# Heads 3 to 14 of a forgetting-attention layer projected by three wide units instead of six narrow ones

## The chip, the cores and the metric

The kernel runs on one core of one Trainium2 chip. The metric is the device time of one execution in microseconds. The engines are TensorE (PE; its weight loads are PEld), VectorE (DVE), ScalarE (ACT), GpSimd (POOL) and SyncE (SP), which issues most DMAs.

## What is computed

Two decoder layers on a sequence of 512 positions and 2048 features, in fp32. Layer 0 is causal forgetting attention with 16 heads of 128, layer 1 is multi-scale retention with 8 heads of 256 (values 512 wide), in chunks of 128. Each layer has one input projection, a SiLU gate, an output projection and a LayerNorm on `ALPHA * h + y`.

```python
# layer 0, x: (1, 512, 2048)
q, k, v, gate, f_logit = split(x @ w_in)              # 4*2048 + 16 columns
q, k = rms_norm(heads(q), q_gain), rms_norm(heads(k), k_gain)
c = cumsum(log_sigmoid(f_logit + b_f))
s = q @ k.T * 128 ** -0.5 + c[:, None] - c[None, :]   # causal
o = softmax(s) @ v
h = layer_norm(ALPHA * x + (o * silu(gate)) @ w_out, ln_gain[0], ln_bias[0])
# layer 1
q, k, v, gate = split(h @ w_in)                       # 2*2048 + 2*4096 columns
q, k = rotary(q), rotary(k) * 256 ** -0.5
o = retention(q, k, v)                                # chunkwise recurrence with decays per head
y = layer_norm(ALPHA * h + (group_norm(o) * silu(gate)) @ w_out, ln_gain[1], ln_bias[1])
```

## The kernel before

All large products are done in fp32 by parts: `split` (L303) makes a high part of an operand on ScalarE (L305) and the rest on VectorE (L306), and `mm3` (L308) sums three matmuls (L310 to L312). A projection is cut into **units**. A `Unit` multiplies the input's four quarters with four quarters of its weights by seven products, p1 to p7, instead of eight (sums of quarters go in, and the outputs are sums of products); a `Plain` unit does the eight. A **narrow** unit has quarters of 256 columns, 512 columns in all; a **wide** one has quarters of 512, 1024 in all. A **block** is the work of one slot on TensorE: 24 matmuls of 256 columns in a narrow unit (14 blocks in a `Unit`), or 12 of 512 columns in a wide one (28 blocks). Each block's weights are one piece of 128x1024, loaded by SyncE (`w_raw`, `w_q`), on some blocks added to another on VectorE (L575), and split.

The seven products pass through three accumulators in PSUM (`acc`, called x, y, z, each two banks). p1, p5 and p6 are copied by ScalarE into a kept tile (L423); later products are added to these (L446 to L468), and four quarters of output come out, named (m, n). A sink takes each. For the first layer's queries and keys that is `Pair.take` (L987): a pair of heads gets its raw queries and keys (`qk_raw`, rooms in0 and in1) by a ScalarE copy (L994) and the sums of squares by four squares per quarter (L999). `normed` then normalizes and transposes them through PSUM, which empties in0 and in1, and `head` does the attention (softmax on ScalarE and VectorE, small PSUM tiles `mmp`, of which there are two). Gates and values of four heads are one wide unit `vg[g]`. The first layer's order is: pair 0 (a `Plain` unit), vg[0], pair 1, vg[1], pairs 2 and 3, vg[2], pairs 4 and 5, vg[3], pair 6, pair 7 (`Plain`). Heads of pairs 6 and 7 ("quick") are worked on side by side. During pair 6's p7 `other_homes` gives the rooms of the input's forms to the forms of the attention's output, and loads and splits one quarter of the input again (`again`).

The second layer goes head by head: a narrow unit for keys and queries, rotated on VectorE (`rope`, L1609 to L1616), and a wide one for values and gates. Head 0's narrow unit is `Plain`, in two halves (L1549), between which the wide unit's first products stand; its results are copied at L1576. The retention's output is scaled on ScalarE (L1753), transposed by TensorE (L1740) and copied out (L1744, L1745).

The order of all engines is fixed when the program is built, by a planner (`Order`): each block on TensorE is one slot, and side work (tasks started with `spawn`) is put in slots by its cost in VectorE and ScalarE time (`need(act=.., dve=..)`), up to 4.4 and 3.8 us of debt. Each room, accumulator and tile of a ring is counted in `free`; a block that needs a room (`require`) makes the planner run the tasks on, within the same slot, until it is free. Weights are loaded up to nine blocks ahead of their product and split two blocks ahead.

## Time and profile before

| | |
|---|---|
| median of 3 runs | 2405.23 us (2400.59 to 2405.72) |
| profiled execution | 2403.45 us, its span 2401.7 us |
| TensorE busy | 2320.4 us, 97% of the span |
| VectorE / ScalarE / GpSimd busy | 1894.4 / 1216.2 / 160.7 us |
| mean granted TensorE clock | 0.988 |
| DMA | 196 GB/s in the mean |

Times in the rows count from the span's start. A matmul's busy time overlaps with the next one's; the step from start to start tells how fast they follow each other. In brackets stands how long an engine was idle before an operation, and what it waited for last.

### The profile page before, as it was taken

To read this page: it belongs to the slowest core of one execution; us is meant where nothing else is said; L and a number is where in the kernel's file an instruction comes from. 1 tells how busy PE (TensorE), PEld (TensorE's weight loads), DVE (VectorE), ACT (ScalarE), POOL (GpSimd) and SP (SyncE) were. 2 spreads that over 40 slices of the span, in tenths; PEclk is the share of its full clock that TensorE was granted. 3 is DMA by queue.
4 is the path that set the end of the run, shared out by engine and by line. 5 is a ranking of instruction groups with operands and counts; after the bars stand their busy time and mean duration, and the time that the engine had idled before them with its cause. 6 is when DMAs were issued, how large, how long until landed. Compare 5 with 4: busy or idle time off the path is not lost.

```text
span 2401.7 us, 34231 instructions
## 1 busy us (share of the span) xinstructions
PE 2320.4 (97%) x13096; PEld 2014.9 (84%) x13096; DVE 1894.4 (79%) x2483; ACT 1216.2 (51%) x1774; POOL 160.7 (7%) x248
## 2 busy tenths in 40 slices
PE   9999999999999999989899999999999999999995
PEld 9888798798799778878779898888889898777784
DVE  5888778678765656679878888898888889987977
ACT  4556556556555534555354545454544445544533
POOL 0000000000000000010020101010101001011002
PEclk9999999999999999999999999999999999999998
DMA  6355544554544467675575857675665659689778
GB/s 225 123 199 175 164 162 159 175 180 153 185 150 156 134 205 233 221 174 154 175 219 194 246 183 220 206 195 187 209 199 193 210 172 265 211 268 292 242 244 190
DMA packets 184564, 471.16 MB, mean 196 GB/s; under 512 B 17968, under 2 KB 63168, under 8 KB 183888
## 3 DMA queue, kind: packets, MB, share of 16 engines
q1 hardware_dynamic: 159136, 395.29, 49.9%
q0 software_dynamic: 25264, 73.69, 12.2%
q8 instruction: 103, 1.69, 0.3%
q14 instruction: 61, 0.50, 0.1%
HBM read 411.20 MB, written 61.91 MB: 197 GB/s over the span
## 4 chain that ended last, share of the span: by engine, by line
PE 44%; DVE 5%; DMA 3%; issue 2%; ACT 1%; POOL 0%; ACTq 0%; DVEq 0%; POOLq 0%
PE acc L310 13%; PE acc L311 13%; PE acc L312 13%; DVE w_l L306 2%; DMA w_raw<-in_wide 2%; PE mmp L310 1%; PE mmp L311 1%; PE mmp L312 1%; DVE w_q L575 1%; ACT w_h L305 1%; PE mmp L1740 0%; DVE z L1840 0%; DMA y_s<-ny 0%; DMA y_s<-y 0%; DMA z_half<-z_in 0%
## 5 line engine op out<-in xcount | busy, mean ns | idle before, releaser
L305 ACT ACTIVATE w_h<-w_q 128x1024 fp32r<-128x1024 f32 x360 | 380.4, 1059 | 425.5 <-DVE w_q L575 218.3
L310 PE MATMUL acc<-w_h,a 128*128 128x512 f32 (+1 forms) x1536 | 551.4, 359 | 6.2 <-DVE kept L468 3.5
L311 PE MATMUL acc<-w_l,a 128*128 128x512 f32 (+1 forms) x1536 | 545.3, 355 | 1.8 <-DVE w_l L306 1.8
L306 DVE TENSOR_TENSOR w_l<-w_raw,w_h 128x1024 fp32r<-128x1024 f32 x314 | 383.4, 1222 | 206.2 <-ACT w_h L305 205.3
L312 PE MATMUL acc<-w_h,a 128*128 128x512 f32 (+1 forms) x1536 | 545.1, 355 | 0.0
L306 DVE TENSOR_TENSOR w_l<-w_q,w_h 128x1024 fp32r<-128x1024 f32 x360 | 439.3, 1221 | 118.1 <-ACT w_h L305 111.1
L310 PE MATMUL acc<-w_h,s 128*128 128x512 f32 (+1 forms) x1408 | 515.9, 366 | 4.3 <-ACT qk_raw L1576 2.1
L311 PE MATMUL acc<-w_l,s 128*128 128x512 f32 (+1 forms) x1408 | 512.0, 364 | 8.0 <-DVE w_l L306 7.9
L312 PE MATMUL acc<-w_h,s 128*128 128x512 f32 (+1 forms) x1408 | 510.1, 362 | 0.0
L305 ACT ACTIVATE w_h<-w_raw 128x1024 fp32r<-128x1024 f32 x314 | 331.7, 1058 | 346.7 <-PE acc L312 161.5
L310 PEld LDWEIGHTS acc<-w_h,a 128*128 128x128 f32 x1536 | 290.9, 189 | 48.3 <-issue 7.4
L311 PEld LDWEIGHTS acc<-w_l,a 128*128 128x128 f32 x1536 | 291.0, 189 | 42.5 <-DVE w_l L306 4.8
L312 PEld LDWEIGHTS acc<-w_h,a 128*128 128x128 f32 x1536 | 290.8, 189 | 41.2
L311 PEld LDWEIGHTS acc<-w_l,s 128*128 128x128 f32 x1408 | 267.6, 190 | 51.4 <-DVE w_l L306 13.6
L310 PEld LDWEIGHTS acc<-w_h,s 128*128 128x128 f32 x1408 | 267.5, 190 | 44.1 <-ACT w_h L305 3.0
L312 PEld LDWEIGHTS acc<-w_h,s 128*128 128x128 f32 x1408 | 267.4, 190 | 41.2
L575 DVE TENSOR_TENSOR w_q<-w_q,w_raw 128x1024 f32<-128x1024 f32 x216 | 263.2, 1220 | 9.0 <-DMA w_raw<-in_wide 6.5
L310 PE MATMUL acc<-a,w_h 128*128 128x256 f32 x464 | 132.9, 287 | 4.3 <-ACT qk_raw L1576 3.1
L312 PE MATMUL acc<-a,w_l 128*128 128x256 f32 x464 | 132.7, 286 | 0.8 <-DVE w_l L306 0.8
L311 PE MATMUL acc<-a,w_h 128*128 128x256 f32 x464 | 132.5, 286 | 0.0
L312 PE MATMUL acc<-s,w_l 128*128 128x256 f32 x448 | 126.8, 283 | 0.0
L311 PE MATMUL acc<-s,w_h 128*128 128x256 f32 x448 | 126.7, 283 | 0.0
(231 smaller groups left out, 2976.3 us busy)
## 6 DMA issues: line engine op xcount, KB each, us to landing
w_raw<-in_wide SPq DMA_DIRECT2D x321, 512.0 KB, 4.0
w_raw<-in_narrow SPq DMA_DIRECT2D x144, 512.0 KB, 3.7
w_q<-in_wide SPq DMA_DIRECT2D x64, 512.0 KB, 4.6
room<-in_wide SPq DMA_DIRECT2D x47, 512.0 KB, 5.0
w_q<-in_narrow SPq DMA_DIRECT2D x26, 512.0 KB, 4.0
y_s<-ny POOLq DMA_DIRECT2D x48, 256.0 KB, 7.0
y_s<-y POOLq DMA_DIRECT2D x40, 256.0 KB, 5.9
room<-in_narrow SPq DMA_DIRECT2D x18, 512.0 KB, 4.5
```

The source lines that it names most:

```text
L305: nc.scalar.activation(h, src, AF.Copy)
L306: nc.vector.tensor_sub(l, src, f32(h))
L310: nc.tensor.matmul(ps, a[0], b[0], start=start, stop=False, skip_group_check=True)
L311: nc.tensor.matmul(ps, a[0], b[1], start=False, stop=False, skip_group_check=True)
L312: nc.tensor.matmul(ps, a[1], b[0], start=False, stop=stop, skip_group_check=True)
L575: nc.vector.tensor_add(u.chain[c], u.chain[c], t)
```

## The change

Three things.

1. Pairs 1 to 6 (heads 3 to 14) come from three wide units, `both[1]`, `both[3]`, `both[5]`, instead of six narrow ones. Each gives pairs i and i+1. The first pair's part is taken as before; the second pair's part is squared for its own sums, and written to DRAM (`parked`) by GpSimd, three quarters from the kept tile, the last by way of a ScalarE copy (`qk_park`). When the first pair's rooms are empty, `fetch` reads it back into them by two loads on SyncE. The order is now both[1], vg[1], both[3], vg[2], both[5], vg[3], pair 7; the attention of both pairs is spawned at the wide unit's p4.
2. `other_homes` runs in vg[3]'s p7, not in pair 6's; its two loads and splits are two tasks, and the quick heads wait for it.
3. In the second layer head 0's narrow unit takes two accumulators, one for each half; and in head 1's wide unit p5 is kept in k1 as in the later heads, no longer in y0, with p2's blocks between those of p1 and p5.

```diff
+SLOW = (("p1", "p2", "+p5"), ("p6",), ("p3", "p7"), ("p4",))
@@ class Pair
+        def has_room(self):
+            return self.raw or fox["emptied"] == self.i and free["in0"] and free["in1"]
...
+        def take_both(self, other, m, n, tile, done):
+
+            def copy():
+                yield need(act=0.5, until=self.has_room)
+                if self.raw is None:
+                    self.new_raw()
+                    self.new_sums()
+                    other.new_sums()
+                    other.parked = [dram.tile([P, 2, 512], F32, name=f"qk_raw{other.i}{i}") for i in range(2)]
+                nc.scalar.activation(self.raw[m][:, :, n * 256:(n + 1) * 256], tile[:, :, :256], AF.Copy)
+                to = other.parked[m][:, :, n * 256:(n + 1) * 256]
+                last = (m, n) == (1, 0)
+                if last:
+
+                    yield need(act=0.5, tmp=1)
+                    t = tmp("qk_park").rearrange("p (e n) -> p e n", e=2)
+                    nc.scalar.activation(t, tile[:, :, 256:], AF.Copy)
+                    nc.gpsimd.dma_start(to, t)
+                    give("tmp", 3)
+                yield need(act=1.2)
+                self.squares(m, n, tile, 0)
+                self.have += 1
+                yield need(act=1.2)
+                other.squares(m, n, tile, 256)
+                if last:
+                    done()
+                else:
+                    nc.gpsimd.dma_start(to, tile[:, :, 256:])
+                    done(3)
+                other.stored += 1
+
+            spawn(copy(), 0)
+
+        def fetch(self):
+            yield need(until=lambda: self.stored == 4 and self.has_room())
+            self.new_raw()
+            for t, d in zip(self.raw, self.parked):
+                nc.sync.dma_start(t, d)
+            yield need(wait=4)
+            self.have = 4
...
             give("in0")
             give("in1")
+            fox["emptied"] = self.i + 1
...
-    qk = [Unit(narrow, i, p.take) for i, p in enumerate(pairs)]
+    both = {i: Unit(wide, 18 + j, partial(pairs[i].take_both, pairs[i + 1]), u2="k2") for j, i in enumerate((1, 3, 5))}
...
-    for i in range(1, 7):
-        qk[i].run(then={"p4": partial(core, i), **({"p7": lambda: other_homes()} if i == 6 else {})})
-        if i in (1, 3, 5):
-            vg[(i + 1) // 2].run()
+    for i in (1, 3, 5):
+        both[i].run(then={"p4": lambda i=i: (core(i), spawn(pairs[i + 1].fetch()), core(i + 1))})
+        vg[(i + 1) // 2].run(then={"p7": lambda: other_homes()} if i == 5 else {})
...
-                self.qk_unit = Plain(narrow, 8, self.take_qk, lambda: [banks[0]] * 2, rows=False)
+                self.qk_unit = Plain(narrow, 2, self.take_qk, lambda: [banks[0], banks[2]], rows=False)
...
-            if h == 1:
-                self.vg_unit.p5 = "y0"
...
-        h.vg_unit.run(leaves=h.h == RH - 1,
+        h.vg_unit.run(SLOW if h.h == 1 else ORDER, leaves=h.h == RH - 1,
                       then={**then, "p4": lambda h=h, last=last: (spawn(h.retain()), last())})
```

The program has 1008 matmuls fewer (13032 before, 12024 now) and 22 DMAs more; the order moves as follows. Line numbers of the changed kernel are higher: the split is L307 and L308, the matmuls L312 to L314.

ScalarE, first layer, the quarters of pair 1 before: copies into `qk_raw`, and four squares per quarter (L999) between high parts of weights (`w_h`).

```order
L994 ACTIVATE qk_raw<-kept 128x2x256
L305 ACTIVATE w_h<-w_raw 128x1024
L999 ACTIVATE kept,rms_ss<-kept 128x128 x4
L994 ACTIVATE qk_raw<-kept 128x2x256
L305 ACTIVATE w_h<-w_q 128x1024
L999 ACTIVATE kept,rms_ss<-kept 128x128 x4
L305 ACTIVATE w_h<-w_q 128x1024 x2
```

The same engine now, the last two quarters of pairs 1 and 2; L1165 and L1170 are the softmax of pair 0's heads.

```order
L1031 ACTIVATE qk_raw<-kept 128x2x256
L1165 ACTIVATE p<-p,sm 128x512
L1170 ACTIVATE p,sm<-p,sm 128x384
L307 ACTIVATE w_h<-w_q 128x1024
L1019 ACTIVATE kept,rms_ss<-kept 128x128 x4
L1031 ACTIVATE qk_raw<-acc 128x2x256
L307 ACTIVATE w_h<-w_q 128x1024
L1019 ACTIVATE kept,rms_ss<-kept 128x128 x4
L1038 ACTIVATE qk_park<-acc 128x512
L1165 ACTIVATE p<-p,sm 128x384
L307 ACTIVATE w_h<-w_q 128x1024
L1019 ACTIVATE acc,rms_ss<-acc 128x128 x4
```

Each quarter has eight squares, four for each pair, and the last one the copy to the tile from which it goes to DRAM.

SyncE now, behind the first wide unit: the second pair's two loads (L1059) among loads of weights (L563).

```order
L563 DMA w_raw<-in_wide 128x1024
L1120 DMA cb<-c_rows 128x512
L563 DMA w_raw<-in_wide 128x1024 x6
L1059 DMA qk_raw<-qk_raw_1866 128x1024
L1059 DMA qk_raw<-qk_raw_1867 128x1024
L563 DMA w_raw<-in_wide 128x1024 x4
```

They stand between two runs of weight loads; before, no queries or keys went through DRAM.

ScalarE, second layer, head 1's wide unit before: `kept` scaled by `gn_r` and `y`, `ny` are head 0's output, `qk_h` the high parts of head 1's rotated keys and queries, L423 the copy of p1.

```order
L305 ACTIVATE w_h<-w_q 128x1024 x6
L1753 ACTIVATE kept<-kept,gn_r 128x512
L305 ACTIVATE qk_h<-rope 128x2x2x256
L1753 ACTIVATE kept<-kept,gn_r 128x512
L305 ACTIVATE qk_h<-rope 128x2x2x256
L1744 ACTIVATE y<-mmp 128x512
L1745 ACTIVATE ny<-mmp 128x512
L1753 ACTIVATE gate<-gate,gn_r 128x512
L423 ACTIVATE kept<-acc 128x1024
```

And now:

```order
L1810 ACTIVATE kept<-kept,gn_r 128x512
L307 ACTIVATE w_h<-w_q 128x1024
L1810 ACTIVATE kept<-kept,gn_r 128x512
L307 ACTIVATE w_h<-w_raw 128x1024
L1801 ACTIVATE y<-mmp 128x512
L1802 ACTIVATE ny<-mmp 128x512
L1810 ACTIVATE gate<-gate,gn_r 128x512
L307 ACTIVATE qk_h<-rope 128x2x2x256
L307 ACTIVATE w_h<-w_q 128x1024 x2
```

High parts of weights, one per block, now stand between the pieces.

TensorE at that place before: the transposes of head 0's output, and the scores of head 1, between two blocks.

```order
L311 MATMUL acc<-w_l,a_9028 128x512
L312 MATMUL acc<-w_h,a_9029 128x512
L1740 MATMUL mmp<-ident,kept 128x128 x8
L310 MATMUL mmp<-qk_h 128x512
L311 MATMUL mmp<-qk_l,qk_h 128x512
L312 MATMUL mmp<-qk_h,qk_l 128x512
```

And now:

```order
L1797 MATMUL mmp<-ident,kept 128x128 x4
L312 MATMUL acc<-w_h,s_8856 128x512
L313 MATMUL acc<-w_l,s_8856 128x512
L314 MATMUL acc<-w_h,s_8857 128x512
L312 MATMUL acc<-w_h,s_8856 128x512
```

A whole block of 12 matmuls follows the first four transposes, before the next four come.

## Rows read from the trace of the kernel before

**Rows 1.** The page: span, and busy time, share and instructions of each engine.
```profile
span 2401.7 us, 34231 instructions
...
PE 2320.4 (97%) x13096; PEld 2014.9 (84%) x13096; DVE 1894.4 (79%) x2483; ACT 1216.2 (51%) x1774; POOL 160.7 (7%) x248
```

**Rows 2.** Windows: us, then PE, PEld, DVE, ACT, POOL busy, PEclk, DMA, GB/s.
```profile
338.30:527.60 189.30, 185.25 (x1179) 164.89 (x1178) 143.50 (x216) 108.46 (x223) 7.54 (x14) 1.00 0.51 166
527.60:716.90 189.30, 185.27 (x1178) 164.90 (x1177) 143.85 (x216) 109.84 (x225) 6.48 (x12) 1.00 0.50 165
...
1188.00:1212.00 24.00, 10.35 (x36) 7.69 (x35) 17.05 (x25) 9.13 (x12) 2.16 (x4) 0.64 0.60 177
1317.00:1341.00 24.00, 24.00 (x116) 19.85 (x115) 23.52 (x25) 16.24 (x22) 6.96 (x12) 1.00 0.64 213
```

**Rows 3.** TensorE's timeline, first layer: start, us, operation, [idle before <-releaser].
```profile
404.35 0.45 PE L310 MATMUL mmp<-qk_h 128*128 128x384 f32 x1 [1.50 <-ACT pT L1096]
```

**Rows 4.** TensorE's timeline, head 0, first wait; the first and last slow spacing.
```profile
1036.20 0.58 PE L310 MATMUL acc<-a,w_h 128*128 128x256 f32 x1 [3.11 <-ACT qk_raw L1576]
...
1039.13 0.28 PE L311 MATMUL acc<-a,w_h 128*128 128x256 f32 x1
```

**Rows 5.** TensorE's timeline, head 0, second wait; first and last slow spacing.
```profile
1062.82 0.67 PE L310 MATMUL acc<-w_h,s 128*128 128x512 f32 x1 [2.05 <-ACT qk_raw L1576]
...
1066.57 0.39 PE L310 MATMUL acc<-w_h,s 128*128 128x512 f32 x1
```

**Rows 6.** TensorE's timeline, head 1's wide unit.
```profile
1188.91 0.39 PE L312 MATMUL acc<-w_h,a 128*128 128x512 f32 x1
1191.06 0.65 PE L1740 MATMUL mmp<-ident,kept 128*128 128x128 f32 x4 [1.76 <-ACT kept L1753]
1196.83 1.12 PE L1740 MATMUL mmp<-ident,kept 128*128 128x128 f32 x4 [5.12 <-ACT kept L1753]
1204.72 0.79 PE L310 MATMUL mmp<-qk_h 128*128 128x512 f32 x1 [6.78 <-ACT ny L1745]
...
1209.90 0.40 PE L310 MATMUL acc<-w_h,s 128*128 128x512 f32 x1
```

**Rows 7.** TensorE's timeline in a narrow unit: first and last of 27 matmuls.
```profile
359.82 0.28 PE L310 MATMUL acc<-w_h,s 128*128 128x256 f32 x1
...
362.94 0.28 PE L312 MATMUL acc<-w_h,s 128*128 128x256 f32 x1
```

**Rows 8.** TensorE's timeline in a wide unit: first and last of 13 matmuls.
```profile
443.74 0.39 PE L312 MATMUL mmp<-qk_h,qk_l 128*128 128x512 f32 x1
...
446.46 0.39 PE L312 MATMUL acc<-w_h,s 128*128 128x512 f32 x1
```

**Rows 9.** Groups by line and shape, ScalarE, 149 to 716.9 us: busy, mean ns.
```profile
L994 ACT ACTIVATE qk_raw<-kept 128x512 f32<-128x512 f32 x18 | 11.0, 620 | 3.8 <-DVE kept L458 2.5 <-DVE kept L463 1.2
```

**Rows 10.** DMA issues, 149 to 773 us: count, KB each, us to landing.
```profile
w_raw<-in_wide SPq DMA_DIRECT2D x64, 512.0 KB, 3.5
...
values<-kept POOLq DMA_DIRECT2D x6, 512.0 KB, 6.1
...
y_raw<-y_a SPq DMA_DIRECT2D x4, 512.0 KB, 6.0
```

**Rows 11.** Waits of SyncE's queue, 149 to 773 us: total, times, longest.
```profile
SPq L561 <- DVE w_q L575: 143.7, 39, 11.5
```

**Rows 12.** ScalarE's and VectorE's timelines, head 0, first wait.
```profile
1035.08 1.07 ACT L1576 ACTIVATE qk_raw<-acc 128x512 f32<-128x512 f32 x2
...
1033.52 1.22 DVE L306 TENSOR_TENSOR w_l<-w_raw,w_h 128x1024 fp32r<-128x1024 f32 x1
```

**Rows 13.** VectorE's and ScalarE's timelines, head 0, second wait.
```profile
1056.07 1.23 DVE L306 TENSOR_TENSOR w_l<-w_q,w_h 128x1024 fp32r<-128x1024 f32 x1 [0.52 <-ACT w_h L305]
...
1061.70 1.06 ACT L1576 ACTIVATE qk_raw<-acc 128x512 f32<-128x512 f32 x2
```

**Rows 14.** ScalarE's timeline, head 1's wide unit.
```profile
1201.12 1.06 ACT L305 ACTIVATE qk_h<-rope 128x1024 fp32r<-128x1024 f32 x1 [4.35 <-DVE rope L1616]
```

More of the change, by code (lines that the diff above doesn't have):

```diff
@@ L909, in split_x @@
         there.add((q, c))
-    fox = dict(heads=0, norms=0)
+    fox = dict(heads=0, norms=0, emptied=0)
     def forget():
@@ L977, in __init__ @@
             self.raw = None
-            self.have = self.scored = 0
+            self.have = self.stored = self.scored = 0
             self.quick = i >= 6
@@ L1003, in take, with new_raw, new_sums, squares @@
             spawn(copy(), 0)
+        def has_room(self):
+            return self.raw or fox["emptied"] == self.i and free["in0"] and free["in1"]
+        def new_raw(self):
+            take("in0")
+            take("in1")
+            self.raw = [pool.tile([P, 2, 512], F32, name="qk_raw", tag=f"in{i}") for i in range(2)]
+        def new_sums(self):
+            self.ss = pool.tile([P, ST, 4], F32, name="rms_ss", tag="rms_ss", bufs=2)
+        def squares(self, m, n, tile, at):
+            for e in range(2):
+                for h in range(2):
+                    v = tile[:, e, at + h * P:at + (h + 1) * P]
+                    nc.scalar.activation(tile[:, e, h * P:(h + 1) * P], v, AF.Square,
+                                         accum_out=self.ss[:, 2 * m + e, 2 * n + h:2 * n + h + 1])
@@ new lines, in take_both @@
+        def take_both(self, other, m, n, tile, done):
+            def copy():
+                yield need(act=0.5, until=self.has_room)
+                if self.raw is None:
+                    self.new_raw()
+                    self.new_sums()
+                    other.new_sums()
[10 more added lines that the diff above has]
+                yield need(act=1.2)
+                self.squares(m, n, tile, 0)
+                self.have += 1
[8 more added lines that the diff above has]
+            spawn(copy(), 0)
@@ L1056, in head @@
             d0, tag_p = self.room[i]
-            turn = (lambda: fox["heads"] >= 2 * self.i) if self.quick else lambda: fox["heads"] == head
+            turn = (lambda: fox["heads"] >= 2 * self.i and fox.get("homes")) if self.quick else lambda: fox["heads"] == head
             yield need(**{d0: 1}, until=lambda: fox.get("forgot") and turn())
@@ L1313, in other_homes, with again @@
                     s4=(HOME["s4"][0], HOME["a11"][1]))
-        def again():
-            for c in range(2):
-                tags = "k2", "k0", "k1"
-                yield need(until=lambda: any(free[t] for t in tags))
-                tag = next(t for t in tags if free[t])
-                take(tag)
-                t = pool.tile([P, 4, 256], F32, name="x_raw", tag=tag)
-                nc.sync.dma_start(t.rearrange("p a b -> p (a b)"), xq[1, 0, c])
-                yield need(dve=1.14, act=0.97, wait=3)
-                if c == 0:
-                    new_form("x21")
-                split_form("x21", t, 4 * c, 4 * c + 4)
-                give(tag)
-            spawn(fetch("a11", "k2", "k0", "k1"))
-        spawn(again(), 1)
+        def again(c):
+            tags = "k2", "k0", "k1"
+            yield need(until=lambda: any(free[t] for t in tags))
+            tag = next(t for t in tags if free[t])
+            take(tag)
+            t = pool.tile([P, 4, 256], F32, name="x_raw", tag=tag)
+            nc.sync.dma_start(t.rearrange("p a b -> p (a b)"), xq[1, 0, c])
+            yield need(dve=1.14, act=0.97, wait=3)
+            split_form("x21", t, 4 * c, 4 * c + 4)
+            give(tag)
+            if c:
+                spawn(fetch("a11", "k2", "k0", "k1"))
+        new_form("x21")
+        for c in range(2):
+            spawn(again(c), 1)
+        fox["homes"] = True
     def late():
@@ L1345, in two_banks @@
         return a, b
-    Plain(narrow, 7, pairs[7].take, two_banks, kind="x").run(
+    Plain(narrow, 1, pairs[7].take, two_banks, kind="x").run(
         BOTH, then={len(BOTH) // 2 - 1: lambda: spawn(fetch("a21", "k2", "k0", "k1")), len(BOTH) - 1: late})
@@ L1548, in __init__ @@
             if h == 0:
[L1549 removed]
+                self.qk_unit = Plain(narrow, 2, self.take_qk, lambda: [banks[0], banks[2]], rows=False)
             else:
[L1551 removed]
+                self.qk_unit = Unit(narrow, 2 + h, self.take_qk, rows=False, u2="y0")
                 if h == 1:
@@ L1910 @@
     part = lambda w, at, n: w[:, at:at + n]
-    pair = lambda i: side(part(fin, 256 * i, 256), part(fin, D + 256 * i, 256))
-    narrow = [pair(i) for i in range(8)]
+    pair = lambda i, n=256: side(part(fin, 256 * i, n), part(fin, D + 256 * i, n))
+    narrow = [pair(i) for i in (0, 7)]
     narrow += [side(part(rin, D + 256 * h, 256), part(rin, 256 * h, 256)) for h in range(RH)]
@@ L1917 @@
     wide += [part(rout[i * D:(i + 1) * D], 1024 * u, 1024) for i in range(2) for u in range(2)]
+    wide += [pair(i, 512) for i in (1, 3, 5)]
     rot, dec = tables()
```

11 lines of the change are left out of this document (1 added, 10 removed).

## The prediction

> **What bounds the kernel now.** I read the page's busy shares first: TensorE is busy 2320.4 of 2401.7 us, VectorE 79% and ScalarE half of the span [rows 1]. So time is TensorE's work plus the places where TensorE waits, and each part of the change is worth what it takes from one of these two. TensorE's work is read from the starts of its matmuls, not from their busy times, since these overlap. Next I read the stages. In the first layer the work repeats every 189.3 us (two narrow units, one wide unit, four heads), TensorE is busy 185.25 us of it at full clock, and VectorE 143.5 and ScalarE 108.5 us [rows 2]: about 4 us per period are waits, of which the row at 404.35 us is typical, an attention matmul that waits 1.50 us until ScalarE has copied a small PSUM tile [rows 3]. In the second layer the timeline shows three larger waits, in head 0 (1036 and 1063 us) and head 1 (1191 to 1205 us) [rows 4, 5, 6]. These three, and the width of the first layer's units, are what the change touches.
>
> **The three wide units.** Removed: 6 narrow units of 14 blocks of 24 matmuls, 2016 matmuls of 256 columns. Added: 3 wide units of 28 blocks of 12, 1008 of 512 columns. Inside a narrow unit 26 spacings take 3.12 us, 0.120 us each [rows 7]; inside a wide one 12 take 2.72 us, 0.2267 us each [rows 8]. So 28 blocks cost 28 x 24 x 0.120 = 80.64 us as two narrow units and 28 x 12 x 0.2267 = 76.17 us as one wide unit: 4.47 us less, three times, **-13.4 us**. TensorE is the bound in all of it, so this lies on the path. The splits of the weights are 128x1024 per block either way and don't change in number.
>
> A rule speaks against this term. The Trainium skill, page "TensorE: Matmul & The Clock Gate", section "Back-to-back issue gap", gives for an isolated matmul a spacing of N/2.4 + 2.5 ns; two of 256 columns would then cost only 2.5 ns more than one of 512, and 1008 times that is 2.5 us instead of 13.4. By that rule the sum below would be 10.9 us higher; the trace disagrees, its two spacings are both some 13 ns above N/2.4.
>
> **The second pair's way through DRAM.** Added per wide unit: four stores of 256 KB on GpSimd's queue, one more ScalarE copy (0.62 us, by the copy that is there already [rows 9]), and two loads of 512 KB on SyncE's queue; the squares and copies of the pairs are as many as before. Nearest rows: 512 KB written to DRAM by GpSimd land in 6.1 us, 512 KB read back by SyncE in 6.0 us [rows 10]. Neither is waited for by TensorE directly: the second pair is read back a dozen and more blocks (over 30 us) after the first is stored, when the first pair's tiles are empty. Behind the loads on SyncE stand weight loads. SyncE's queue has held such loads back for up to 11.5 us in this layer already [rows 11], and loads are issued up to nine blocks ahead, 9 x 2.72 = 24 us, of which a load uses 3.5 [rows 10]. A fetch may thus wait 20 us for nothing. I put it at **0**, at most 2 us for each of the three.
>
> **Waits of the first layer.** The two pairs' attention now starts together behind one wide unit, the same 4 heads per period. VectorE's load is 76% of a period now and would be 143 of 184.8 us, 77%; ScalarE's goes from 57% to 59%. ScalarE's work is denser behind a wide unit, because each quarter brings eight squares instead of four; by the planner's order and the durations of the rows its backlog there grows from 2.3 to 4.1 us at most. Against blocks of 2.72 us with splits two blocks ahead that is near the edge. Some waits grow, others have a different neighbour. Bounds: all 4 us per period vanish (-12 for three) or they double (+12); I take **+1**. Moving the forms' change of homes from the last narrow unit to the last gates' unit moves two splits (1.2 us of VectorE and 1.06 of ScalarE each) and two loads to a place at the same load: 0, within 2.
>
> **Head 0's banks.** The two halves of its query-key unit used one accumulator; now each has its own. First wait: the second half stands 3.11 us for the copies of the first half's result, then 13 spacings at the lower clock, 2.93 us instead of 1.56 [rows 4], together 4.5. The copies that held the accumulator run at 1035.08, but the next block's low part is subtracted only from 1033.52 to 1034.74 [rows 12]: with a free accumulator TensorE next waits for that. So about 1.5 us of the wait go, with some of the slow spacings: **-2.0** (0.5 to 3.5 us). Second wait, p5 of the wide unit for the second half's copies: 2.05 us idle, and 9 spacings in 3.75 us instead of 2.04 [rows 5]; the low part there had been ready since 1057.3, and only the copies at 1061.70 were missing [rows 13]. Nothing is late next: **-3.9** (3 to 4 us).
>
> **Head 1's p5 in another room.** In the kernel before, p5 of head 1's wide unit needed room y0, which two pieces of earlier work still held; the planner pressed all of that work, head 0's last four transposed groups and head 1's rotations and their splits, into one block. TensorE ends its last matmul before that about 1189.1 and starts normal work at 1204.72; between lie only eight transposes, at most 0.12 us each [rows 6], so 15.6 - 0.9 = 14.7 us idle. VectorE and ScalarE work in turns there: the split of the second rotated part ends on ScalarE at 1202.18 [rows 14]. Then 12 spacings at the lower clock take 5.18 instead of 2.72 us [rows 6]: 2.5 more. Together 17.2 us. In the changed kernel the same work is spread over eleven blocks, with no more than 4.5 us of VectorE in any. How that fares is shown by the same place in head 2 (1317 to 1341 us): VectorE busy 23.52 of 24.00 us, TensorE without an idle moment, clock 1.00 [rows 2]. But here VectorE gets 39.0 us (counted over the order, by the rows' durations) in blocks that take TensorE 36.2; its backlog reaches 4.9 us where head 2 reaches 4.2, and the splits are two blocks, 5.4 us, ahead. I leave 1 us of waits: **-16.2** (10 to 17).
>
> **Sum.** -13.4 + 0 + 1 - 2.0 - 3.9 - 16.2 = -34.5 us. The profiled execution took 2403.45 us (span 2401.7), so 2369.0; it lies 1.8 us under the median of the runs, so 2370.7 against that. I say **2370**.
>
> **Rivals.**
> 1. *The wait of head 1 moves.* k1, p5's new room, is freed only once the rotation has read head 1's second pair, and ScalarE's copy into it would stand in front of the splits. For it: VectorE's backlog of 4.9 us at just that place. Against: head 2 does this at nearly the same density without a wait. It would give back 5 to 10 us: 2375 to 2380, taken as 2377.
> 2. *The first layer becomes bound by ScalarE and VectorE.* If each period's waits grow by 5 us (4.1 us of backlog, and the typical wait of 1.5 us three times over), 15 us return: about 2385. For it: two pairs' squares, norms and softmax steps now come in one bunch, and a PSUM bank with the last quarter stays held for about ten ScalarE instructions. Against: average loads of 77% and 59%.
> 3. *Slower.* The fetch waits on SyncE for the transposes that empty the first pair's tiles, and all weight loads stand behind it. It costs nothing up to about 20 us of waiting; to turn -34.5 into a loss, each of three fetches would have to hold the queue some 12 us beyond that, 32 us. Price at 35 us: 3 x (35 - 20) = +45, 2415. For it: SyncE waited 11.5 us for VectorE already [rows 11]. Against: the order puts the fetch behind the emptying tiles' last reader with blocks to spare.
> 4. *Width brings only 2.5 ns per pair of matmuls.* As a mechanism here: the new blocks would run at 0.2375 us a matmul, where the old wide ones show 0.2267 [rows 8]; 2381. By the page named above it would be so; the rows bear it out in no block.
> 5. *It doesn't do what it says*: the planner places the mends where another ring makes them wait, and only the width pays: 2390.
>
> **How the numbers follow.** Forecast 0.66 (2357 to 2376), rival 1 0.12, rival 2 0.12, rival 3 0.04, rival 4 0.01, rival 5 0.05. The range takes the forecast with its bounds, -12 and -2 of the first layer's waits and the mends at the low end, and rival 1 and the nearer part of rival 2 at the high end: 2355 to 2384. 0.2%, 4.8 us, is about what a measurement of this kernel can tell from no change. Faster by more: 0.94, all cases but rival 3 and the far tail of rival 5, to which I give 0.02 within. Slower: 0.04, rival 3.
>
> **What would show it.** The period of the first layer at about 184.8 us plus what its waits changed; 512-column spacing of 0.227 us in the new units; no TensorE wait over 2 us near the second layer's first units and clock 1.00 there; head 1's wide unit as long as head 2's to 1 us. Wrong it would be if rows with waits for a fetched pair, for SyncE's loads or for ScalarE's copies in the first layer add up to more than 10 us, or if head 1's p5 waits for k1.

## The result and the profile after

The changed kernel takes 2382.59 us (median of 4 runs, 2381.26 to 2384.26) against 2405.02 (2400.59 to 2405.72): a ratio of 0.9911, interval 0.9894 to 0.9928. It is 22 us faster; 34.5 were forecast. The time lies inside the range, at its upper end, and 12 us of the gain that the sum gave are missing. The forecast's own bounds ended at 2376; the range reached 2384 because rival 1 and part of rival 2 were added to it. Neither came about as it was described, so that the range holds the time is in part luck.

The page of the changed kernel, the lines that answer to [rows 1]:

```profile
span 2381.5 us, 32252 instructions
...
PE 2304.4 (97%) x12088; PEld 1955.2 (82%) x12088; DVE 1893.1 (79%) x2474; ACT 1212.8 (51%) x1756; POOL 168.9 (7%) x260
```

Where the 20.2 us between the two spans went is found by cutting both timelines at the same blocks (start of the first matmul of each; us):

| stretch | before | after | difference |
|---|---|---|---|
| first period: pairs 1 and 2, vg[1] | 190.3 | 189.5 | -0.8 |
| second period: pairs 3 and 4, vg[2] | 189.7 | 189.0 | -0.7 |
| third period: pairs 5 and 6, vg[3] | 189.3 | 194.8 | +5.5 |
| pair 7 | 54.8 | 60.2 | +5.5 |
| first output projection, LayerNorm, up to head 0 | 205.3 | 200.9 | -4.4 |
| head 0's units and head 1's narrow unit | 196.8 | 189.7 | -7.1 |
| head 1's wide unit | 100.2 | 82.9 | -17.3 |
| all the rest | 1126.0 | 1125.0 | -1.0 |

So the second layer gave 24 us, and the first layer, where TensorE has 13.4 us less to do, became 5 us longer. The windows of the changed kernel for the three periods and the middle of head 1's wide unit (us; PE, PEld, DVE, ACT, POOL busy; PEclk; DMA; GB/s), which answer to [rows 2]:

```profile
149.40:338.90 189.50, 181.21 (x829) 146.07 (x828) 150.85 (x234) 109.69 (x218) 7.64 (x13) 0.99 0.53 178
338.90:527.90 189.00, 181.44 (x839) 146.33 (x838) 144.33 (x213) 107.72 (x217) 9.25 (x16) 1.00 0.55 178
527.90:722.70 194.80, 184.78 (x844) 149.60 (x843) 144.78 (x213) 108.21 (x215) 9.29 (x16) 0.98 0.50 169
...
1171.10:1210.00 38.90, 38.90 (x181) 32.24 (x180) 38.21 (x59) 25.87 (x33) 10.36 (x16) 1.00 0.67 217
```

In the second period TensorE is busy 181.44 us where it was 185.25, so the width is there; but it is idle 7.6 us where it was 4.05. In head 1 the idle time is gone. TensorE's waits by what ended them, 149.4 to 783 us (total, times, longest), the five largest, and behind them the two largest of the kernel before (149.3 to 773.4 us):

```profile
PE mmp L1132 <- ACT pT L1155: 4.5, 4, 2.3
PE acc L313 <- DVE w_l L308: 3.9, 4, 1.1
PE mmp L1091 <- DVE sm L1181: 3.8, 1, 3.8
PE mmp L1277 <- DVE sm L1181: 2.9, 2, 1.5
PE mmp L1132 <- DVE qk_l L1083: 2.6, 2, 2.2
```

```profile
PE mmp L310 <- ACT pT L1096: 4.6, 3, 1.6
PE mmp L1073 <- ACT pT L1096: 2.1, 8, 0.3
```

Four of the five are waits of small products (`mmp`) for ScalarE or VectorE. Over the whole lists the waits that a step of ScalarE ended last fall from 9.0 to 6.2 us, and those that a step of VectorE ended last (`sm`, `qk_l`, `o`, `kept`, `w_l`) rise from 3.3 to 19.0. The timelines show where: these are TensorE's small products, ScalarE's copies and VectorE's steps at the end of vg[2] and the start of the next wide unit.

```profile
513.81 0.60 PE L1100 MATMUL mmp<-ident,qk_raw 128*128 128x128 f32 x4
...
521.09 0.60 PE L1132 MATMUL mmp<-ident,p 128*128 128x128 f32 x4
522.75 0.63 PE L1100 MATMUL mmp<-ident,qk_raw 128*128 128x128 f32 x4 [1.06 <-DVE sm L1171]
527.62 0.55 PE L1132 MATMUL mmp<-ident,p 128*128 128x128 f32 x3 [1.48 <-ACT pT L1155]
530.76 0.60 PE L1100 MATMUL mmp<-ident,qk_raw 128*128 128x128 f32 x4
536.36 0.87 PE L1132 MATMUL mmp<-ident,p 128*128 128x128 f32 x3 [2.23 <-DVE qk_l L1083]
```

```profile
523.42 0.47 ACT L1082 ACTIVATE qk_h<-mmp,cols 128x256 fp32r<-128x256 f32 x1 [0.26 <-PE mmp L1100]
525.42 0.47 ACT L1082 ACTIVATE qk_h<-mmp,cols 128x256 fp32r<-128x256 f32 x1 [1.53 <-DVE qk_l L1083]
...
526.99 0.58 ACT L1155 ACTIVATE pT<-mmp 128x512 f32<-128x512 f32 x1
```

```profile
523.78 1.22 DVE L308 TENSOR_TENSOR w_l<-w_q,w_h 128x1024 fp32r<-128x1024 f32 x1
524.91 0.48 DVE L1083 SCALAR_TENSOR_TENSOR qk_l<-mmp,cols,qk_h 128x256 fp32r<-128x256 f32 x1
```

L1100 transposes the second pair (pair 4, just fetched), L1132 the softmax's result for pair 3's second head; the two alternate. Each group holds one of the two small PSUM tiles (`mmp`) until ScalarE and VectorE have taken it in turns: copy, subtraction, copy, subtraction. VectorE does its first subtraction (524.91) behind a PSUM addition and a split, so ScalarE stands 1.53 us in the middle of the group, and the copy of pT, for which TensorE waits at 527.62, stands behind it.

### The profile page after: what moved, and what is told of

It is laid out like the page before. It is cut to its first block, busy times and chain, and to the rows that moved or that the text cites. A ratio compares the mean times of both kernels' runs of the same rounds, so it can differ in the third digit from the quotient of the medians.

```text
span 2381.5 us, 32252 instructions
## 1 busy us (share of the span) xinstructions
PE 2304.4 (97%) x12088; PEld 1955.2 (82%) x12088; DVE 1893.1 (79%) x2474; ACT 1212.8 (51%) x1756; POOL 168.9 (7%) x260
## 4 chain that ended last, share of the span: by engine, by line
PE 52%; DVE 7%; DMA 5%; issue 3%; ACT 3%; POOL 0%; DVEq 0%; ACTq 0%; SPq 0%; POOLq 0%
PE acc L312 16%; PE acc L314 16%; PE acc L313 16%; DVE w_l L308 2%; DMA w_raw<-in_wide 2%; ACT w_h L307 2%; PE mmp L312 1%; PE mmp L313 1%; PE mmp L314 1%; DMA v_sum<-in_wide 1%; DVE w_q L577 1%; PE mmp L1797 1%; PE mmp L1277 0%; DMA y_s<-ny 0%; DVE z L1897 0%
## 5 line engine op out<-in xcount | busy, mean ns | idle before, releaser
L307 ACT ACTIVATE w_h<-w_q 128x1024 fp32r<-128x1024 f32 x360 | 380.7, 1059 | 433.6 <-DVE w_q L577 232.8
L308 DVE TENSOR_TENSOR w_l<-w_raw,w_h 128x1024 fp32r<-128x1024 f32 x314 | 383.6, 1222 | 195.2 <-ACT w_h L307 193.8
L312 PE MATMUL acc<-w_h,a 128*128 128x512 f32 (+1 forms) x1392 | 528.5, 380 | 6.8 <-DVE kept L470 4.8
L308 DVE TENSOR_TENSOR w_l<-w_q,w_h 128x1024 fp32r<-128x1024 f32 x360 | 439.7, 1222 | 109.4 <-ACT w_h L307 100.7
L313 PE MATMUL acc<-w_l,a 128*128 128x512 f32 (+1 forms) x1392 | 521.3, 375 | 2.1 <-DVE w_l L308 1.9
L314 PE MATMUL acc<-w_h,a 128*128 128x512 f32 (+1 forms) x1392 | 520.8, 374 | 0.0
L307 ACT ACTIVATE w_h<-w_raw 128x1024 fp32r<-128x1024 f32 x314 | 331.8, 1058 | 359.3 <-PE acc L314 168.4
L313 PE MATMUL acc<-w_l,s 128*128 128x512 f32 x1216 | 476.1, 392 | 12.2 <-DVE w_l L308 12.0
L312 PE MATMUL acc<-w_h,s 128*128 128x512 f32 x1216 | 479.7, 394 | 2.5 <-ACT w_h L307 2.5
L314 PE MATMUL acc<-w_h,s 128*128 128x512 f32 x1216 | 474.5, 390 | 0.0
L312 PEld LDWEIGHTS acc<-w_h,a 128*128 128x128 f32 x1392 | 263.5, 189 | 55.3 <-issue 8.7
L313 PEld LDWEIGHTS acc<-w_l,a 128*128 128x128 f32 x1392 | 263.7, 189 | 49.0 <-DVE w_l L308 6.1
L314 PEld LDWEIGHTS acc<-w_h,a 128*128 128x128 f32 x1392 | 263.3, 189 | 47.1
L313 PEld LDWEIGHTS acc<-w_l,s 128*128 128x128 f32 x1216 | 228.6, 188 | 64.7 <-DVE w_l L308 20.4
L312 PEld LDWEIGHTS acc<-w_h,s 128*128 128x128 f32 x1216 | 228.5, 188 | 48.7 <-ACT w_h L307 3.8
L314 PEld LDWEIGHTS acc<-w_h,s 128*128 128x128 f32 x1216 | 228.3, 188 | 48.1
L314 PE MATMUL acc<-a,w_l 128*128 128x256 f32 x464 | 131.7, 284 | 1.7 <-DVE w_l L308 1.7
L312 PE MATMUL acc<-a,w_h 128*128 128x256 f32 x464 | 131.6, 284 | 1.5 <-ACT w_h L307 1.5
L314 PE MATMUL acc<-s,w_l 128*128 128x256 f32 x448 | 126.8, 283 | 0.0
```

The source lines that it names most:

```text
L307: nc.scalar.activation(h, src, AF.Copy)
L308: nc.vector.tensor_sub(l, src, f32(h))
L312: nc.tensor.matmul(ps, a[0], b[0], start=start, stop=False, skip_group_check=True)
L313: nc.tensor.matmul(ps, a[0], b[1], start=False, stop=False, skip_group_check=True)
L314: nc.tensor.matmul(ps, a[1], b[0], start=False, stop=stop, skip_group_check=True)
```

## The experiments

All times are medians of 4 runs or more, each with its ratio to the kernel before on the same chip. The runs are spread over several chips, on which the kernel before took 2402.8 to 2406.5 us, so a difference between two medians is good to some 3 us. The stretch behind head 1 alone takes between 1123.7 and 1130.6 us in the traces, without any edit there. Where small differences matter, the same stretch of two traces is therefore compared too.

**The two parts apart.** e1_mends is the kernel before with the second layer's part alone:

```diff
-                self.qk_unit = Plain(narrow, 8, self.take_qk, lambda: [banks[0]] * 2, rows=False)
+                self.qk_unit = Plain(narrow, 8, self.take_qk, lambda: [banks[0], banks[2]], rows=False)
...
-            if h == 1:
-                self.vg_unit.p5 = "y0"
...
-        h.vg_unit.run(leaves=h.h == RH - 1,
+        h.vg_unit.run(SLOW if h.h == 1 else ORDER, leaves=h.h == RH - 1,
```

> The kernel before with the third part of the change alone: head 0's two accumulators, head 1's p5 in k1 with p2's blocks between. Theory W (the two traces side by side: the wide units save 13.4 us of TensorE but the first layer's waits grow by 20, so the first layer pays nothing, and the whole gain is the mends: head 0's blocks 7.2 us shorter, head 1's 17.2): 2405.0 - 24.4 = 2380.6, as fast as the changed kernel (2382.6) or a little faster. Rival F (the forecast's own terms: mends -22.1, wide units -12.4): 2383, with the first layer's first stretch, 149 to 773 us, as before; but then the changed kernel should have been at 2370. Both agree on the mends within 2 us; W falls if this run is above 2390.

2380.22 us, ratio 0.9898 (0.9882 to 0.9913). e2_wide undoes the same lines in the changed kernel:

> The changed kernel without its third part: head 0's narrow unit in one accumulator, head 1's p5 in y0 in the old order; the wide units and the forms' move stay. Theory W: 2382.6 + 24.4 = 2407, no faster than the kernel before (2405). Rival F (wide units worth 12 us, which something in the mends gave back): 2393.

2406.57 us, ratio 1.0011 (1.0002 to 1.0021): no faster than before. So the whole gain of the change is the second layer's few lines, and the three wide units, as they stood, bring nothing. e7_head1 has head 1's lines only:

> The kernel before with head 1's mend alone (p5 in k1, p2's blocks between). By the traces of before and after head 1's blocks lost 17.2 us of waits: 2402.8 to 2405 less 17.2 = 2386 to 2388, and head 0's two accumulators make the rest up to e1_mends (2380), 6 to 7 us. Rival (the two depend on one another): above 2392 or below 2383.

2388.14 us, ratio 0.9928 (0.9913 to 0.9943), 16.7 us under the kernel before; up to e1_mends 7.9 are left for head 0's accumulators (7.2 by the ratios). In its trace head 1's wide unit takes 82.3 us and head 0's stretch 196.5, as before, so the one part does not hang on the other.

**Is it the way through DRAM?** e4_notrip leaves out the twelve stores, and its fetch loads something that waits for no store; heads 5, 6, 9, 10, 13 and 14 work on other numbers.

```diff
-                    nc.gpsimd.dma_start(to, t)
...
-                    nc.gpsimd.dma_start(to, tile[:, :, 256:])
...
-            for t, d in zip(self.raw, self.parked):
-                nc.sync.dma_start(t, d)
+            for i, t in enumerate(self.raw):
+                nc.sync.dma_start(t.rearrange("p a b -> p (a b)"), wide[0, 0, 0, i])
```

> The changed kernel without the way through DRAM: the stores of the second pairs are left out, and the fetch loads two pieces of a weight instead, so that it waits for no store; heads 5, 6, 9, 10, 13 and 14 thus work on other numbers in the same amount. Theory W with M or L (no wait of TensorE comes from the stores or the fetch): 2382.6 within 3 us. Rival T (part of the 20 us is the round trip, by the kept tiles' later release or by DMA traffic): 2375 or less.

2383.16 us: unchanged. The round trip costs nothing that can be measured.

**The second pair's place.** In e3_later the second pair is normalized and transposed only after the first pair's attention:

```diff
-            yield need(until=lambda: self.have == 4 and fox["norms"] == self.i)
+            yield need(until=lambda: self.have == 4 and fox["norms"] == self.i
+                       and (self.i not in (2, 4, 6) or fox["heads"] >= 2 * self.i))
```

> The changed kernel; the second pair of each wide unit (pairs 2, 4, 6) is normalized and transposed only when both heads of the first pair are through their softmax. Theory M (the waits come where the second pair's transposes and the first pair's attention stand side by side and share the two small PSUM tiles, at the end of the gates' unit and the start of the next): the first layer's waits fall from 43 to some 25 us, 2382.6 - 15 = 2367, with the stretch 149 to 783 us some 15 us shorter. Rival L (it is the load of VectorE in the gates' unit's last products, whichever tasks make it): waits move but keep their sum, 2378 to 2390.

2365.32 us, ratio 0.9832 (0.9818 to 0.9847): 17.3 us faster than the changed kernel, and faster than both kernels that the case compares. Its windows, three periods:

```profile
149.80:333.80 184.00, 179.35 (x821) 145.40 (x820) 144.49 (x214) 107.72 (x215) 7.62 (x13) 0.99 0.56 183
333.80:515.80 182.00, 180.89 (x842) 146.97 (x840) 143.34 (x213) 107.20 (x215) 8.16 (x14) 1.00 0.54 181
515.80:701.10 185.30, 181.67 (x842) 146.86 (x841) 145.08 (x215) 109.52 (x221) 9.67 (x17) 1.00 0.53 178
```

The second period is 7 us shorter than in the changed kernel, with nearly the same busy times; only the idle time has gone. At the same place TensorE's attention now runs by itself, with waits of 0.26 and 0.36 us where they were 1.06 to 2.23:

```profile
507.74 0.60 PE L1133 MATMUL mmp<-ident,p 128*128 128x128 f32 x4
...
511.89 0.55 PE L1133 MATMUL mmp<-ident,p 128*128 128x128 f32 x3 [0.36 <-ACT pT L1156]
515.46 0.55 PE L1133 MATMUL mmp<-ident,p 128*128 128x128 f32 x3 [0.26 <-ACT pT L1156]
```

e8_all_later gives the same condition to all pairs, 1 to 7.

> The changed kernel with every pair from 1 to 7 normalized and transposed only when the heads of the pair before are through their softmax. Theory M: the first pairs' transposes are mostly later than that anyway, so 2361 to 2366, like e3_later or a little less. Rival (attention then runs late, and the end of the first layer or a full room makes TensorE wait): above 2370.

2366.79 us (2365.81 to 2373.25): like e3_later, just above its forecast. The odd pairs were not in the way.

**What is it at that place: load, turns or tiles?** Three kernels put idle work back into e3_later where the transposes had been. e5_load: ScalarE and VectorE work in the same amount, on the two halves of a row of the raw tile one after the other, so that ScalarE's second copy need not wait for VectorE.

```diff
+            if self.i in (2, 4, 6):
+                yield need(until=lambda: self.have == 4 and fox["norms"] == self.i)
+                for s in range(ST):
+                    yield need(act=0.75, dve=0.7)
+                    for h in range(2):
+                        v = self.raw[s // 2][:, s % 2, h * 256:(h + 1) * 256]
+                        nc.scalar.activation(v, v, AF.Copy)
+                        nc.vector.tensor_scalar(v, v, 1.0, None, op0=ALU.mult)
```

> e3_later with idle work put where the second pair's transposes were taken from: when the second pair is in, four steps of two ScalarE copies and two VectorE multiplications by one, 128x256 each, on its raw tile (values unchanged), in place of the two copies and two subtractions of each of the four transposed groups. No PSUM tile and no TensorE work in it. Theory M (the two small PSUM tiles, shared by the transposes and the attention, made the waits): at most 4 us more than e3_later's 2365.3, so 2365 to 2370. Rival L (it was VectorE's and ScalarE's load there): most of the 17 us come back, 2378 or more.

2366.17 us: the load alone is worth 1 us by the medians, and 2.9 by the traces (table below). e9_tiles does it on a small PSUM tile that TensorE has filled, with the old group's shape of turns:

```diff
+                        t = mmp()
+                        for h in range(2):
+                            nc.tensor.transpose(t[:, h * P:(h + 1) * P], self.raw[s // 2][:, s % 2, h * P:(h + 1) * P], ident)
...
+                        for h in range(2):
+                            nc.scalar.activation(last[:, :256], last[:, :256], AF.Copy)
+                            nc.vector.tensor_scalar(last[:, :256], last[:, :256], 1.0, None, op0=ALU.mult)
+                        give("mmp")
```

> e3_later with an idle copy of the old transposes at their old place: when the second pair is in, four groups of two transposes of its raw tile into a small PSUM tile (its 128 columns twice, half of a real group), and one slot later two ScalarE copies and two VectorE multiplications by one of that tile in place, whose result nobody reads. TensorE gets 3 x 4 x 2 x 0.11 = 2.6 us more. Theory M (sharing the two small PSUM tiles with the attention makes the waits): 2365.3 + 2.6 and most of the 17 us, 2378 to 2388. Rival (neither load nor tiles; it was the moment at which the pair's attention could begin): 2366 to 2370.

2381.82 us: 16.5 us come back, of which 2.6 are the idle transposes' own. Its waits on TensorE in the first layer are of the changed kernel's kind again (149.5 to 782 us, the largest three):

```profile
PE mmp L1150 <- ACT pT L1173: 7.3, 7, 2.3
PE mmp L1150 <- DVE o L1309: 1.9, 1, 1.9
PE mmp L312 <- ACT pT L1173: 1.7, 2, 1.3
```

e9_tiles differs from e5_load in two things, the tiles and the turns. e11_turns has the turns alone, with the same order of operations on TensorE, ScalarE and VectorE as e5_load:

```diff
-                    for h in range(2):
-                        v = self.raw[s // 2][:, s % 2, h * 256:(h + 1) * 256]
+                    v = self.raw[s // 2][:, s % 2, :256]
+                    for h in range(2):
                         nc.scalar.activation(v, v, AF.Copy)
```

> e5_load with one thing changed: the two ScalarE copies and the two VectorE multiplications of a step now work in turns on the same 128x256 of the raw tile, so that the second copy waits for the first multiplication, as the second qk_h copy of a transposed group waits for the first subtraction (1.53 us at 525.42 in the changed kernel). No PSUM tile. e9_tiles had both, e5_load neither. Theory M (the small PSUM tiles being held is what costs): 2365 to 2369, like e5_load. Theory C (ScalarE, waiting for VectorE's turn, holds up the attention's copies queued behind it): 2375 to 2384, like e9_tiles.

2373.41 us, between the two forecasts: 7.2 us above e5_load, 8.4 under e9_tiles. e12_parts comes from the other side: it takes the turns out of the changed kernel.

```diff
-                for i, gain in ((0, gq), (2, gk)):
-                    h, l = (p[:, i:i + 2, s * P:(s + 1) * P] for p in self.qk)
+                parts = [(i, gain, *(p[:, i:i + 2, s * P:(s + 1) * P] for p in self.qk)) for i, gain in ((0, gq), (2, gk))]
+                for i, gain, h, l in parts:
                     nc.scalar.activation(h, t[:, i:i + 2], AF.Copy, scale=gain)
+                for i, gain, h, l in parts:
                     nc.vector.scalar_tensor_tensor(l, t[:, i:i + 2], gain, f32(h), op0=ALU.mult, op1=ALU.subtract)
```

> The changed kernel with the two ScalarE copies of a transposed group (query and key high parts) issued before its two VectorE subtractions, in place of copy, subtraction, copy, subtraction; in all pairs; the places in the order stay. Theory C (the second copy's wait for VectorE in the middle of the group is what costs): 2368 to 2376. Theory M (the group's and the attention's tiles together are too many for two): 2380 to 2383, unchanged.

2372.79 us, 9.8 us under the changed kernel. On each of the three engines the operations stand in the same order in both kernels. What differs is the order in which the program issues them: in the changed kernel the second copy, into one part of the tile `qk_h`, waits for the first subtraction, which reads another part of it; no value needs this wait. The groups by line show that the turns were what it removed; ScalarE's `qk_h` copies in the changed kernel (338.9 to 722.7 us) and in e12_parts (330 to 712 us), the idle time before them behind the second bar:

```profile
L1082 ACT ACTIVATE qk_h<-mmp,cols 128x256 fp32r<-128x256 f32 x34 | 16.0, 470 | 33.7 <-DVE qk_l L1083 24.9 <-PE mmp L1091 8.5 <-PE mmp L1100 0.3
```

```profile
L1082 ACT ACTIVATE qk_h<-mmp,cols 128x256 fp32r<-128x256 f32 x34 | 14.1, 465 | 9.1 <-PE mmp L1092 8.9 <-PE mmp L1101 0.3
```

24.9 us in which ScalarE stood for VectorE's subtraction are gone. The traces can be compared by the stretch from the start of the first period to head 0, which holds all that these edits touch:

| kernel | us |
|---|---|
| e3_later | 814.1 |
| e5_load (load) | 817.0 |
| e11_turns (load and turns) | 821.6 |
| e9_tiles (load, turns, tiles) | 831.4 |
| changed kernel | 834.5 |
| e12_parts (changed kernel without the turns) | 820.8 |

So both turns and tiles are at work, but their shares are not settled: the turns are worth 7 to 10 us of the 17 by the medians, and by the traces 4.6 (put in) to 13.7 (taken out) of 20.3. From e11_turns to e9_tiles it is 9.8 us, of which 2.6 are the idle transposes; but the planner counts the small tiles, so the order of operations changes there too, and the tiles' waits are not told apart from that. The one kernel that has the tiles without the turns is e12_parts, 7.5 us above e3_later (6.6 by the traces). It was not tried whether e12_parts and e3_later together give more than e3_later.

**What the width is worth by itself.** For that the narrow kernel has to be without such waits too. e6_narrow_later is e1_mends with e3_later's condition.

> e1_mends (narrow units, both mends) with the same later normalization of pairs 2, 4 and 6 as in e3_later. Tells what the width is worth when the attention stands alike. Theory W+M (width is worth up to 13.4 us once its waits are gone; the narrow kernel too has some of these waits, row 404.35 and its like): 2370 to 2379, that is 5 to 13 us slower than e3_later. Rival (the later normalization alone makes the gain and the width is worth nothing): 2365 to 2367.

2380.09 us, the same as e1_mends and outside both forecasts. But the run tells nothing of the width: in the narrow kernel it is the odd pairs whose transposes alternate with the attention, and the condition for pairs 2, 4 and 6 left the order of operations on TensorE, ScalarE and VectorE exactly as it was. e10_narrow_all has the condition for all pairs, after which no transposes stand among the attention:

> e1_mends (narrow units, both mends) with every pair normalized and transposed only after the heads of the pair before are through their softmax. In e6_narrow_later the delay of pairs 2, 4 and 6 had left the order nearly as it was, since in the narrow kernel it is pairs 3 and 5 whose transposes stand among the attention; here no transposes stand there in any pair, as in e3_later, so the two differ by the width alone. Theory W+M: 2370 to 2379, 5 to 13 us above e3_later (2365.3), and below e1_mends (2380.2). Rival 1 (the width is worth nothing in like orders): 2365 to 2367. Rival 2 (the narrow kernel's waits are not of this kind): 2380.

2372.77 us, ratio 0.9863 (0.9847 to 0.9880): 7.5 us under e1_mends, so the narrow kernel had the same kind of wait, and 7.5 above e3_later. Its windows against those of e3_later above:

```profile
149.00:337.40 188.40, 183.43 (x1165) 163.93 (x1164) 147.78 (x221) 109.10 (x213) 5.95 (x11) 1.00 0.50 171
337.40:524.10 186.70, 185.41 (x1182) 165.56 (x1181) 144.20 (x216) 108.99 (x221) 6.47 (x12) 1.00 0.49 170
524.10:710.40 186.30, 185.04 (x1178) 165.16 (x1177) 142.82 (x215) 110.77 (x225) 6.47 (x12) 1.00 0.49 167
```

Against e3_later a wide unit saves 4.4 and 4.7 us in the first two periods, and 1.0 in the third. But e3_later delays only pairs 2, 4 and 6. The wide kernel with the same condition as e10_narrow_all is e8_all_later, 6.0 us under it; its periods take 181.9, 186.1 and 185.2 us in the profiled execution (the longest of its four), which is 6.5, 0.6 and 1.1 us less. How much attention falls into a period differs between these orders, so no single period gives the price of the width. Together the three periods save 10.1 us (e3_later) or 8.2 (e8_all_later), and up to head 0 it is 7.2 or 3.6.

## Why the prediction was right and wrong, step by step

- **The bound, and the place of the three large waits**: right. TensorE is 97% busy in both, and each term but the first layer's waits was worth about what it was taken to take from TensorE's work or waits.
- **The three wide units, -13.4**: the unit price was right. The new units run at the wide spacing (ten spacings in 2.27 us, TensorE's timeline in both[3], as in [rows 8]); that two periods of e3_later give 4.4 and 4.7 us where 4.47 were worked out agrees with it, but is in part chance, since e8_all_later gives 6.5 and 0.6:

```profile
349.77 0.39 PE L313 MATMUL acc<-w_l,s 128*128 128x512 f32 x1
...
352.04 0.40 PE L314 MATMUL acc<-w_h,s 128*128 128x512 f32 x1
```

  The Trainium skill's formula for an isolated matmul (page "TensorE: Matmul & The Clock Gate", section "Back-to-back issue gap") would have given, as an estimate, 0.8 us per unit; the spacings of the trace disagree, 0.120 us at 256 columns and 0.227 at 512. By that formula the narrow matmul would be the shorter one (an estimate of 0.109 us), and not the wide one the longer, so rival 4's 0.2375 us is not what the formula gives. In sum e3_later is 7.5 us below e10_narrow_all and e8_all_later 6.0, not 13.4; for e3_later the rest is in the third period and pair 7, below.
- **The way through DRAM, 0**: right, by e4_notrip. The loads landed in 5.0 us and the stores in 2.7, where 6 was taken; SyncE had no wait at the fetch itself (L1059). The weight loads of the wide units (L563) waited at most 9.3 us, for a low part, within the 20 that were free; SyncE's longest wait, 14.5 us, stood at a weight load of pair 7 (L718). The changed kernel's DMA groups (149 to 783 us), and these two waits of SyncE:

```profile
qk_raw<-qk_raw SPq DMA_DIRECT2D x6, 512.0 KB, 5.0
...
qk_raw<-kept POOLq DMA_DIRECT2D x9, 256.0 KB, 2.7
```

```profile
SPq L563 <- DVE w_l L308: 145.2, 46, 9.3
...
SPq L718 <- DVE w_l L308: 48.0, 8, 14.5
```

- **Waits of the first layer, +1 (-12 to +12)**: this step failed: the waits grew by 20 us, outside its bounds, and that is more than all that is missing, since some 5 us came back elsewhere (the sum, below). Counted over the starts (each step beyond the spacing of its width, between the start of the first period and the end of pair 7), the waits grew from 22.9 to 43.2 us. The step reasoned from two sums, the average load of VectorE and ScalarE and their backlog. Neither explains these waits: e3_later has the same loads and is 17 us faster, and e5_load adds the load without the wait. It is a chain: a transposed group that ScalarE and VectorE take in turns, the attention's copies behind it on ScalarE, two small tiles for both, and the projection's matmuls behind TensorE's waiting product. The row shown for the typical wait [rows 3] was one end of such a chain (a pT copy), and the prediction did not ask what had held that copy up; the change put pair i+1's transposes, by the fetch, exactly beside pair i's attention. The prediction's sign of being wrong missed it too: it counted waits for a fetched pair, for SyncE's loads and for ScalarE's copies, and these stay under 10 us (6.2 for ScalarE), while those for VectorE grew to 19.0.
- **Rival 2** had the right place and nearly the right size (about 15 us, 2385), but not the cause: it blamed squares, norms and softmax in one bunch, and e3_later keeps all that work, and loses the waits by moving only the second pair's norms and transposes behind the attention.
- **The forms' change of homes, 0 within 2**: not tried alone. The third period, in which it now stands, is 5.8 us longer than the second, and in e3_later 3.3; pair 7 is 5.5 longer than before, and 4.4 come back behind it. From e10_narrow_all to e3_later all up to head 0 gained 7.2 us, where three units should give 13.4; so some 6 us went in the third period and behind it. In the longest wait of the first layer, TensorE's 3.76 us up to 713.16, one of the moved splits takes part: VectorE does it right before the softmax step that TensorE waits for.

```profile
710.46 1.22 DVE L308 TENSOR_TENSOR x<-x_raw,x 128x1024 fp32r<-128x1024 f32 x1
```

  How much of the 6 us is this work and how much the last pairs' attention stays open.
- **Head 0's accumulators, -5.9**: the mechanism was right, -7.1 by the blocks' starts (-7.9 by the medians of e7_head1 and e1_mends, -7.2 by their ratios). The second wait went whole, 3.9 us (its rows add up to 3.8). Of the first wait and its slow spacings 2.9 us went where 2.0 were taken. Some 1 us of the 7.1 has nothing to do with the change: at the start of head 0's unit two short waits of like length (0.8 and 1.2 us) were followed by the lower clock in the kernel before (granted 0.78 from 978.6 to 983 us) and by the higher one in the changed kernel (1.00 from 983.8 to 988); other steps took nearly as much back. The waits in head 0 that are left (984 to 1085 us) are those for VectorE's low parts and ScalarE's high parts, as was said, and one for ScalarE on the forms of the second layer's input (`raw`); `qk_raw` is not among them:

```profile
PE acc L314 <- DVE w_l L308: 1.7, 2, 0.9
PE acc L312 <- ACT w_h L307: 1.5, 2, 1.3
PE mmp L1535 <- ACT raw L1553: 1.2, 1, 1.2
PE acc L313 <- DVE w_l L308: 0.9, 2, 0.6
```

- **Head 1's p5, -16.2**: right, 16.7 by e7_head1 and 17.3 by the starts. The 1 us that was left for VectorE's backlog was not needed, and rival 1 did not occur: VectorE is busy 38.21 of 38.90 us there (above), and TensorE has no idle moment. The transposes that were pressed into one block stand apart now:

```profile
1181.74 0.60 PE L1797 MATMUL mmp<-ident,kept 128*128 128x128 f32 x4
1184.95 0.60 PE L1797 MATMUL mmp<-ident,kept 128*128 128x128 f32 x4
```

- **The sum**: with the measured sizes, -13.4 + 20.3 for the first layer, -7.1 and -17.3 for the heads, 2.5 of TensorE's work moved into the first layer, -4.4 behind it and -1.0 in the rest: -20.4, against -20.2 of the spans.

## What to carry to other kernels

A faster unit on the bounding engine is worth its arithmetic only if the small work between its blocks keeps its own place: when two chains of small steps (here one pair's transposes and another's attention) come to stand side by side and share two PSUM tiles and two engines in turns, the bounding engine waits although no other engine is near full. To forecast such a change, look for what is newly interleaved in the order, and follow one short wait of the kind back through the queues, rather than adding up loads. Of two engines that work on one tile in turns, let the first do all its steps before the second begins; where a chain can start later without being needed sooner, start it later.

## What the runs showed of the hardware

The length of a short wait does not by itself tell at which clock TensorE goes on. In the changed kernel the matmuls behind the waits of 1.06 and 1.48 us (522.75 and 527.62, above) kept the spacing of the higher clock, while behind 2.23 us (536.36) and behind 3.76 us (713.16) they ran at the lower one, 0.427 us a matmul of 512 columns. The granted clock was 0.50 from 536.9 to 539.5 us and 0.52 behind the longer wait; over the whole third period, where both stand, the mean is 0.98. TensorE's timeline behind the longer one, and its window:

```profile
713.16 0.78 PE L1091 MATMUL mmp<-ident,qk_raw 128*128 128x128 f32 x4 [3.76 <-DVE sm L1181]
...
715.02 0.63 PE L312 MATMUL acc<-w_h,a 128*128 128x512 f32 x1
715.45 0.63 PE L313 MATMUL acc<-w_l,a 128*128 128x512 f32 x1
...
717.08 0.39 PE L314 MATMUL acc<-w_h,a 128*128 128x512 f32 x1
```

```profile
713.60:717.10 3.50, 3.50 (x12) 2.77 (x10) 1.61 (x3) 2.57 (x4) 0.00 (x0) 0.52 0.00 0
```

From 713.60 to 717.08 eight spacings take 3.48 us instead of 1.81, so this wait cost 1.7 us more than its own length. But a wait of 2.20 us, at the same transposes and for the same step of VectorE, was followed by the higher clock in e3_later (1.00) and by the lower one in e8_all_later (0.50), first in e3_later:

```profile
720.98 0.63 PE L1092 MATMUL mmp<-ident,qk_raw 128*128 128x128 f32 x4 [2.20 <-DVE qk_l L1084]
```

```profile
720.90:724.00 3.10, 3.02 (x26) 3.05 (x27) 1.30 (x3) 0.95 (x2) 0.00 (x0) 1.00 0.03 5
```

And in e8_all_later:

```profile
721.82 1.09 PE L1091 MATMUL mmp<-ident,qk_raw 128*128 128x128 f32 x4 [2.20 <-DVE qk_l L1083]
```

```profile
721.80:724.90 3.10, 3.08 (x15) 3.10 (x16) 0.91 (x3) 0.95 (x2) 0.00 (x0) 0.50 0.02 5
```

In the same way a wait of 2.3 us for a pT copy early in the first period was followed by seven slow spacings in the changed kernel (at 251.58) and by none in e12_parts (at 249.19). What decides between the two is not shown here. For a forecast, a wait of about 2 us in such a place costs its own length, or 1.2 to 1.7 us more.
